# RWKV head pairs: both heads' A products and the two low-rank products on 64 rows of the array each

## The chip, the cores and the metric

The kernel runs on one core of a Trainium2 chip. The time is device microseconds of one execution. Engines are named as the profile names them: PE is TensorE, PEld its weight loads, DVE VectorE, ACT ScalarE, POOL GpSimd, SP SyncE. PSUM is the memory that matmuls write; a bank holds 512 fp32 values on each of 128 partitions.

## What is computed

One inference step of one decoder layer for 512 prompt tokens and 64 sample tokens (8 sequences of 8). RWKV-7 time mixing with 8 heads of 64 and differential attention with 4 heads run as parallel branches on the same normalised input, are merged by gates, and an MLP follows. The change lies in the RWKV branch:

```python
r, k, v, wd, ad, gd = jnp.split(Pr, RWKV_SPLITS, axis=-1)
w = -jax.nn.softplus(-(lp['w0'] + jnp.tanh(wd) @ lp['w2'])) - 0.5
decay = jnp.exp(-jnp.exp(w))
a = jax.nn.sigmoid(lp['a0'] + ad @ lp['a2'])
kk = hs(k * lp['k_k']); kk = kk / norm(kk)
k = k * (1.0 + (a - 1.0) * lp['k_a'])
# one step of the scan, for every head:
sa = einsum('bhij,bhj->bhi', S, -kk_t)
S = S * w_t + sa * (kk_t * a_t) + v_t * k_t
y_t = einsum('bhij,bhj->bhi', S, r_t)
```

`wd` and `ad` have 64 columns each. `w2` and `a2` are the two low-rank weights.

## The kernel before

The 576 tokens are 9 chunks of 64: eight of the prompt, one of the samples. Heads go in pairs; `rwkv(hp)` (L742 on) is a generator that prepares one head pair, `hp` 0 to 3, in stages. A tile has 128 partitions: 64 of the even head (`par` 0) and 64 of the odd head (`par` 1). `chain(pr)` (L987) then carries the state of two head pairs through the nine chunks (`pch`, `pY`). Below that run the dense products of the layer, the so-called fills: `ps_z`, `ps_g` and the like, products of 128x128 weights with 288 tokens. `fill` and `take` hand a given number of them to the PE between the steps of `rwkv`; the rest of the order comes from the scheduler that builds the program, which places each instruction by priority and by when it takes its inputs to be ready. Every engine then runs its instructions strictly in that order.

The steps that the texts name, in the order of one head pair:

- `pn`, `nr`, `nb` (L755 to L763): norms of `kk`. POOL raises `nr` to a power and copies it out to `nb`, which `pk` (L790) needs.
- `pw`, `pa` (L767 to L773): the low-rank products, in two halves of 288 tokens. `wl` holds w2 in rows 0 to 63 and zeros below; `al` holds zeros in rows 0 to 63 and a2 below. Both multiply the whole tile `Pt[12]`, which holds tanh(wd) above and ad below. ACT evacuates them into `u` and `aa`.
- DVE and ACT scans and products up to `rkp`, which `pbn` (L807) needs, and to `KB` and `ST` (L811 to L821). `KB` holds both heads, on their own partitions. `ST[par]` holds one head on its own 64 partitions; POOL sets the other 64 to zero (L818), so that a product over all 128 partitions sums that head alone.
- `pA` (L825 to L836): for each head nine products of `KB` with `ST[par]`, in groups of 4, 4 and 1 chunks, one bank for each group. DVE multiplies by masks: the head's own rows into `ABR`, the other rows into the zero half of `ST`.
- `pV` and `SVU`, `pK` and `KBt` (L843 to L855): transposes by PE, evacuated by ACT. POOL puts identity blocks and zeros into `SVU` and zeros into `TT` (L871, L872, L923, L924).
- `pI` (L861), then the inverse of a triangular block in 32x32 products (`pW`, `pZ`, L876 to L905), and `pF` (L937), which takes `vm`, made by POOL in three buffers.

PSUM: `bank` is a ring of three banks, `tbank` one, `cbank(0)` and `cbank(1)` one each (the chain's `pch` and `pY`), and two more belong to the fills.

Of the kernel before, what the change touches and what calls it, by code (L numbers as in the profile page):

```python
# [8 lines left out]
F32 = mybir.dt.float32  # L9
# [6 lines left out]
P = 128  # L16
# [25 lines left out]
def tile_hybrid_step(ctx, tc, xT, xsT, ktab, vtab, s0T, ptab, w_in, vecs, w2a2, g2, lamv,  # L42
                     w_bra, w_brb, w_out, w_up, w_down, cst, bias_p, bias_s,
                     yT, kTo, vTo, Sp, Ss, sh):
    nc = tc.nc
# [25 lines left out]
    def mm(out, lhsT, rhs, start=True, stop=True):  # L71
        ring["mm"] = PE.matmul(out=out, lhsT=lhsT, rhs=rhs, start=start, stop=stop)  # L72
        return ring["mm"]
# [27 lines left out]
    def bank(name):  # L101
        return psw.tile([P, 512], F32, tag="w", name=name)

    def tbank(name):
        return psc.tile([P, 512], F32, tag="t", name=name)
# [211 lines left out]
    ka2 = rc.tile([P, 8], F32, name="ka2")  # L317
    ts(ka2[:, 0:4], v(V_KA, 4), 0.5, MUL, 0.0, ADD, GE)
    ts(ka2[:, 4:8], v(V_KA, 4), -0.5, MUL, 1.0, ADD, GE)

    wl = rc.tile([P, 512], F32, name="wl")
    al = rc.tile([P, 512], F32, name="al")
    GE.memset(wl[64:128], 0.0)
    GE.memset(al[0:64], 0.0)
    wg = rc.tile([P, 512], F32, name="wg")
    reset = rc.tile([P, NT], F32, name="reset")
    GE.memset(reset, 1.0)
# [87 lines left out]
    with tc.issue_after(behind.ins):  # L415
        nc.sync.dma_start(out=pti, in_=ptab)
        nc.sync.dma_start(out=lv, in_=lamv)
        nc.sync.dma_start(out=bp, in_=bias_p)
        nc.sync.dma_start(out=bs, in_=bias_s)
        nc.sync.dma_start(out=wl[0:64], in_=w2a2[0:64])  # L420
        nc.sync.dma_start(out=al[64:128], in_=w2a2[64:128])
        nc.sync.dma_start(out=wg, in_=g2)

    def shifted(i):
# [317 lines left out]
    def rwkv(hp):  # L742
# [5 lines left out]
        def tmp(tag, bufs=1):  # L748
            return rt.tile([P, NT], F32, tag="T", name=f"{tag}_{hp}", bufs=6)
# [14 lines left out]
                       in_=nr.rearrange("p (a o) -> p a o", o=1).broadcast_to([P, 10, 64]))  # L764
        u = tmp("u")
        aa = tmp("aa")
        for t0, n in HALF:  # L767
            pw = bank(f"pw{hp}{t0}")
            mm(pw[:, :n], wl[:, hs], Pt[12][:, t0:t0 + n])
            act(u[:, t0:t0 + n], pw[:, :n], AF.Tanh, scale=0.5, bias=hw0[:, hp:hp + 1])  # L770
            pa = bank(f"pa{hp}{t0}")
            mm(pa[:, :n], al[:, hs], Pt[12][:, t0:t0 + n])
            act(aa[:, t0:t0 + n], pa[:, :n], AF.Tanh, scale=0.5, bias=hw0[:, 4 + hp:5 + hp])  # L773
        (fill if hp != 2 else take)(8)
        ts(u, u, 1.0, ADD)
# [38 lines left out]
        for par, rows in halves:  # L814
            stt(KB[rows, :, par], ch(aa)[rows], 0.5, ch(pinv)[rows], MUL, MUL)
            tt(KB[rows, :, 1 - par], ch(k2)[rows], ch(pinv)[rows], MUL)
            st = rb_.tile([P, NCH, 2, 64], F32, tag=f"ST{par}", name=f"ST{par}_{hp}")
            GE.memset(st[64 - 64 * par:128 - 64 * par], 0.0)  # L818
            stt(st[rows, :, 0], ch(kk)[rows], -1.0, ch(pm)[rows], MUL, MUL)
            tt(st[rows, :, 1], ch(r)[rows], ch(pe)[rows], MUL)  # L820
            ST.append(st)  # L821
# [1 line left out]


        ABR = rb_.tile([P, NCH, 2, 64], F32, tag="ABR", name=f"ABR{hp}")  # L825
        for par in range(2):
            rows = slice(64 * par, 64 * par + 64)
            oth = slice(64 - 64 * par, 128 - 64 * par)
            for c0, cn, mk in ((0, 4, C_M), (4, 4, C_M), (8, 1, C_MS)):
                pA = bank(f"pA{hp}{par}{c0}")  # L830
                for i in range(cn):
                    mm(pA[:, i * P:(i + 1) * P], KBc[c0 + i], ST[par][:, c0 + i])
                pAv = pA[:, :cn * P].rearrange("p (c w) -> p c w", c=cn)
                f2 = lambda a: a[:, c0:c0 + cn].rearrange("p c a t -> p c (a t)")
                tt(f2(ABR)[rows], pAv[rows], m3(c[rows, mk:mk + P], cn), MUL)
                tt(f2(ST[par])[oth], pAv[oth], m3(c[oth, mk:mk + P], cn), MUL)  # L836
# [647 lines left out]
```

## Time and profile before

| | |
|---|---|
| time, median of 3 | 1004.05 us (1003.92 to 1005.98) |
| profiled execution | 1006.88 us, of which its span 1005.1 us |
| mean granted TensorE clock | 0.993 |
| busy PE / PEld | 975.1 us (97%) / 919.4 us (91%) |
| busy DVE / ACT / POOL | 688.9 (69%) / 497.0 (49%) / 87.5 us (9%) |
| DMA | 105.75 MB, mean 105 GB/s |

The profile is that of one execution. Its page gives busy times, the chain that ended last and the costliest groups. Behind it stands the trace, which answers questions: what an engine did in a stretch (the timeline), who waited for whom (waits), and busy time, clock and DMA by stretch (windows). A timeline row gives start, duration of the merged group, engine, line, operation, out<-in, the tile of the PE array in rows*columns, and the shape. Each fp32 product of the RWKV steps is two records (passes) there, and their ends overlap, so the distance between starts, not the duration of one, is what a pass costs.

### The profile page before, as it was taken

What the parts mean: (1) busy time and instruction counts of PE and PEld (TensorE: products, weight loads), DVE (VectorE), ACT (ScalarE), POOL (GpSimd) and SP (SyncE); (2) the same over time, 40 slices, a digit from 0 to 9 for tenths busy, and PEclk for the clock granted to TensorE, in tenths of its full rate; (3) what the DMA queues carried; (4) which work ended last, traced back from release to release, by engine and by line L of the source; (5) the groups of instructions that cost most, each with busy time, mean ns of one, the idle gap of its engine ahead of it and who ended that gap; (6) DMA issues with size and microseconds to landing.
All of it is one profiled execution on the core that took longest, in us unless ns stands there. A gap on an engine that the chain in (4) does not pass through costs nothing.

```text
span 1005.1 us, 24415 instructions
## 1 busy us (share of the span) xinstructions
PE 975.1 (97%) x10012; PEld 919.4 (91%) x10012; DVE 688.9 (69%) x1459; ACT 497.0 (49%) x1094; POOL 87.5 (9%) x171
## 2 busy tenths in 40 slices
PE   9999999899999998999989999999999999999996
PEld 9999998898887887988779999999999999999996
DVE  6698566864946679444579898966666666666644
ACT  6576455354435355453334666644444444444732
POOL 2511001301010340000210000000000000000001
PEclk9999999999989999999999999999999999999999
DMA  7422673211111234323357642222222222221402
GB/s 266 136 70 83 205 223 114 61 64 45 43 59 45 69 106 152 104 81 113 103 182 225 206 140 86 83 95 85 88 92 85 85 84 85 84 87 41 135 3 95
DMA packets 50833, 105.75 MB, mean 105 GB/s; under 512 B 6066, under 2 KB 8114, under 8 KB 50594
## 3 DMA queue, kind: packets, MB, share of 16 engines
q1 hardware_dynamic: 47442, 96.95, 30.4%
q0 software_dynamic: 1648, 5.35, 1.5%
q8 instruction: 79, 1.29, 0.5%
q10 hardware_dynamic: 1632, 1.89, 0.5%
q14 instruction: 32, 0.26, 0.1%
HBM read 89.38 MB, written 14.78 MB: 104 GB/s over the span
## 4 chain that ended last, share of the span: by engine, by line
PE 83%; DVE 6%; ACT 4%; issue 3%; DMA 2%; POOL 1%; SPq 0%; DVEq 0%; ACTq 0%; POOLq 0%
PE ps_dn L72 20%; PE ps_g L72 8%; PE ps_z L72 8%; PE ua L1220 5%; PE ux L1220 5%; PE ps_wo L72 4%; PE ps_k L72 3%; PE uc L1220 3%; PE ub L1220 3%; PE ud L1220 2%; PE ps_bra L72 2%; PE ps_q L72 2%; PE pch L72 2%; PE ps_brb L72 2%; PE ps_v L72 2%
## 5 line engine op out<-in xcount | busy, mean ns | idle before, releaser
L72 PE MATMUL ps_dn<-q,hi_dn 128*128 128x288 f32 x768 | 154.7, 296 | 0.0
L72 PEld LDWEIGHTS ps_dn<-q,hi_dn 128*128 128x128 f32 x768 | 122.7, 188 | 1.4
L72 PE MATMUL ps_dn<-q,lo_dn 128*128 128x288 f32 x384 | 113.2, 295 | 0.0
L72 PE MATMUL ps_g<-xl,hi_g 128*128 128x288 f32 x256 | 79.7, 311 | 0.0
L72 PE MATMUL ps_g<-xh,hi_g 128*128 128x288 f32 x256 | 79.0, 309 | 0.0
L72 PE MATMUL ps_g<-xh,lo_g 128*128 128x288 f32 x256 | 79.0, 309 | 0.0
L72 PEld LDWEIGHTS ps_dn<-q,lo_dn 128*128 128x128 f32 x384 | 72.0, 188 | 0.0
L72 PE MATMUL ps_z<-xh,lo_z 128*128 128x288 f32 (+1 forms) x224 | 68.9, 308 | 0.0
L72 PE MATMUL ps_z<-xh,hi_z 128*128 128x288 f32 (+1 forms) x224 | 67.6, 302 | 0.0
L72 PE MATMUL ps_z<-xl,hi_z 128*128 128x288 f32 (+1 forms) x224 | 66.8, 298 | 0.0
L61 DVE TENSOR_TENSOR ya<-ya,ps_dn 128x288 f32<-128x288 f32 x96 | 43.2, 451 | 29.4 <-PE ps_dn L72 29.4
L58 ACT ACTIVATE hi_dn<-raw_dn 128x512 fp32r<-128x512 f32 x48 | 30.1, 628 | 57.0 <-PE ps_dn L72 57.0
L1220 PE MATMUL ua<-h_b,hi 128*128 128x288 f32 x256 | 53.2, 298 | 0.0
L1220 PE MATMUL ux<-h_t,hi 128*128 128x288 f32 x256 | 52.3, 296 | 0.0
L58 ACT ACTIVATE c<-c 128x288 f32<-128x288 f32 x112 | 48.4, 439 | 7.4 <-DVE c L61 5.8
L72 PEld LDWEIGHTS ps_g<-xh,hi_g 128*128 128x128 f32 x256 | 48.7, 190 | 3.1 <-issue 1.8
L72 PEld LDWEIGHTS ps_g<-xl,hi_g 128*128 128x128 f32 x256 | 48.6, 190 | 1.9
L72 PEld LDWEIGHTS ps_g<-xh,lo_g 128*128 128x128 f32 x256 | 48.6, 190 | 1.6 <-DVE lo_g L61 0.2
L58 ACT ACTIVATE hi<-a 128x1024 fp32r<-128x1024 f32 (+1 forms) x32 | 27.1, 846 | 42.0 <-PE ps_dn L72 34.2
L72 PE MATMUL ps_dn<-q,w 128*128 128x320 f32 (+1 forms) x336 | 46.3, 297 | 0.0
L61 DVE TENSOR_TENSOR lo<-s,hi 128x1024 fp32r<-128x1024 f32 x32 | 39.2, 1224 | 10.1 <-ACT hi L58 10.0
L72 PEld LDWEIGHTS ps_dn<-q,w 128*128 128x128 f32 x336 | 45.3, 190 | 0.1
(395 smaller groups left out, 2802.2 us busy)
## 6 DMA issues: line engine op xcount, KB each, us to landing
a<-in_w_up_dram SPq DMA_DIRECT2D x32, 512.0 KB, 3.4
raw_dn<-in_w_down_dram SPq DMA_DIRECT2D x64, 256.0 KB, 2.8
raw_g<-in_w_in_dram SPq DMA_DIRECT2D x32, 256.0 KB, 3.1
raw_z<-in_w_in_dram SPq DMA_DIRECT2D x28, 256.0 KB, 3.1
gt_d<-gg SPq DMA_DIRECT2D x16, 288.0 KB, 2.4
g<-gt_d SPq DMA_DIRECT2D x16, 288.0 KB, 3.6
kp<-in_ktab_dram SPq DMA_DIRECT2D x16, 256.0 KB, 4.5
vp<-in_vtab_dram SPq DMA_DIRECT2D x16, 256.0 KB, 3.8
```

What stands on the lines that cost most here:

```text
L58: ring["act"] = AE.activation(out=out, in_=in_, func=func, **kw)
L61: ins = (eng or VE).tensor_tensor(out=out, in0=a, in1=b, op=op)
L72: ring["mm"] = PE.matmul(out=out, lhsT=lhsT, rhs=rhs, start=start, stop=stop)
L1220: ring["mm"] = PE.matmul(out=ps[:, :288], lhsT=l[:, k], rhs=hb[blk][:, h, k], start=start and i == 0, stop=i == 11, skip_group_check=skip)
```

## The change

`wl` and `al` become one tile `wa`, loaded by one DMA, with no zeros. `pw` uses rows 0 to 63 of `wa` and `Pt[12]`, `pa` rows 64 to 127; the two are written in turn, `pa` to a bank of its own, and each is told to come after the product before it. For `pA` the loops change places: for each group of chunks, the products of both heads are written in turn, each on its own 64 rows of `KB` and `ST`, into two banks. The ring of three, `tbank` and both `cbank`s supply them. The zero memsets of `ST` go.

```diff
--- before.py
+++ after.py
@@ -317,11 +317,7 @@
     ka2 = rc.tile([P, 8], F32, name="ka2")
     ts(ka2[:, 0:4], v(V_KA, 4), 0.5, MUL, 0.0, ADD, GE)
     ts(ka2[:, 4:8], v(V_KA, 4), -0.5, MUL, 1.0, ADD, GE)
-
-    wl = rc.tile([P, 512], F32, name="wl")
-    al = rc.tile([P, 512], F32, name="al")
-    GE.memset(wl[64:128], 0.0)
-    GE.memset(al[0:64], 0.0)
+    wa = rc.tile([P, 512], F32, name="wa")
     wg = rc.tile([P, 512], F32, name="wg")
     reset = rc.tile([P, NT], F32, name="reset")
     GE.memset(reset, 1.0)
@@ -417,8 +413,7 @@
         nc.sync.dma_start(out=lv, in_=lamv)
         nc.sync.dma_start(out=bp, in_=bias_p)
         nc.sync.dma_start(out=bs, in_=bias_s)
-        nc.sync.dma_start(out=wl[0:64], in_=w2a2[0:64])
-        nc.sync.dma_start(out=al[64:128], in_=w2a2[64:128])
+        nc.sync.dma_start(out=wa, in_=w2a2)
         nc.sync.dma_start(out=wg, in_=g2)
 
     def shifted(i):
@@ -764,12 +759,15 @@
                        in_=nr.rearrange("p (a o) -> p a o", o=1).broadcast_to([P, 10, 64]))
         u = tmp("u")
         aa = tmp("aa")
+
         for t0, n in HALF:
             pw = bank(f"pw{hp}{t0}")
-            mm(pw[:, :n], wl[:, hs], Pt[12][:, t0:t0 + n])
+            nm = f"pa{hp}{t0}"
+            pa = bank(nm) if t0 == 0 else tbank(nm) if hp == 2 else cbank(1, nm)
+            for ps, rows in ((pw, slice(0, 64)), (pa, slice(64, 128))):
+                with tc.issue_after(ring["mm"].ins):
+                    mm(ps[:, :n], wa[rows, hs], Pt[12][rows, t0:t0 + n])
             act(u[:, t0:t0 + n], pw[:, :n], AF.Tanh, scale=0.5, bias=hw0[:, hp:hp + 1])
-            pa = bank(f"pa{hp}{t0}")
-            mm(pa[:, :n], al[:, hs], Pt[12][:, t0:t0 + n])
             act(aa[:, t0:t0 + n], pa[:, :n], AF.Tanh, scale=0.5, bias=hw0[:, 4 + hp:5 + hp])
         (fill if hp != 2 else take)(8)
         ts(u, u, 1.0, ADD)
@@ -815,7 +813,6 @@
             stt(KB[rows, :, par], ch(aa)[rows], 0.5, ch(pinv)[rows], MUL, MUL)
             tt(KB[rows, :, 1 - par], ch(k2)[rows], ch(pinv)[rows], MUL)
             st = rb_.tile([P, NCH, 2, 64], F32, tag=f"ST{par}", name=f"ST{par}_{hp}")
-            GE.memset(st[64 - 64 * par:128 - 64 * par], 0.0)
             stt(st[rows, :, 0], ch(kk)[rows], -1.0, ch(pm)[rows], MUL, MUL)
             tt(st[rows, :, 1], ch(r)[rows], ch(pe)[rows], MUL)
             ST.append(st)
@@ -823,14 +820,17 @@
 
 
         ABR = rb_.tile([P, NCH, 2, 64], F32, tag="ABR", name=f"ABR{hp}")
-        for par in range(2):
-            rows = slice(64 * par, 64 * par + 64)
-            oth = slice(64 - 64 * par, 128 - 64 * par)
-            for c0, cn, mk in ((0, 4, C_M), (4, 4, C_M), (8, 1, C_MS)):
-                pA = bank(f"pA{hp}{par}{c0}")
-                for i in range(cn):
-                    mm(pA[:, i * P:(i + 1) * P], KBc[c0 + i], ST[par][:, c0 + i])
-                pAv = pA[:, :cn * P].rearrange("p (c w) -> p c w", c=cn)
+
+        for c0, cn, mk in ((0, 4, C_M), (4, 4, C_M), (8, 1, C_MS)):
+            two = [cbank(par, f"pA{hp}{par}{c0}") if c0 == 4 else tbank(f"pA{hp}{par}{c0}")
+                   if c0 and par and hp < 3 else bank(f"pA{hp}{par}{c0}") for par in range(2)]
+            for i in range(cn):
+                for par, rows in halves:
+                    mm(two[par][:, i * P:(i + 1) * P], KB[rows, c0 + i].rearrange("p a t -> p (a t)"),
+                       ST[par][rows, c0 + i].rearrange("p a t -> p (a t)"))
+            for par, rows in halves:
+                oth = slice(64 - 64 * par, 128 - 64 * par)
+                pAv = two[par][:, :cn * P].rearrange("p (c w) -> p c w", c=cn)
                 f2 = lambda a: a[:, c0:c0 + cn].rearrange("p c a t -> p c (a t)")
                 tt(f2(ABR)[rows], pAv[rows], m3(c[rows, mk:mk + P], cn), MUL)
                 tt(f2(ST[par])[oth], pAv[oth], m3(c[oth, mk:mk + P], cn), MUL)
```

How the scheduler then orders the instructions is seen in the programs themselves. Numbers at the end of a name tell instances apart; `pA004` is head pair 0, head 0, chunks from 4 on; x4 are four products in a row.

On PE, head pair 0, at the A products, before:

```order
L72 MATMUL pA000_2825<-ST0_0_2814,KB0_2810 128x128 x4
L72 MATMUL pA004_2832<-ST0_0_2814,KB0_2810 128x128 x4
L72 MATMUL pA008_2839<-ST0_0_2814,KB0_2810 128x128
L72 MATMUL ps_z9_0_3032<-xh_103,lo_z9_1_3029 128x288
L72 MATMUL ps_z9_0_3032<-xh_103,hi_z9_1_3028 128x288
L72 MATMUL ps_z9_0_3032<-xl_104,hi_z9_1_3028 128x288
L72 MATMUL ps_z9_0_3032<-xh_103,lo_z9_1_3029 128x288
L72 MATMUL pA010_2843<-ST1_0_2820,KB0_2810 128x128 x4
L72 MATMUL ps_z9_0_3032<-xh_103,hi_z9_1_3028 128x288
L72 MATMUL ps_z9_0_3032<-xl_104,hi_z9_1_3028 128x288
L72 MATMUL ps_z9_0_3032<-xh_103,lo_z9_1_3029 128x288
L72 MATMUL pA014_2850<-ST1_0_2820,KB0_2810 128x128 x4
```

and after the change (`pA004` x4 stands alone, two `pbn` products and eight fills ahead of these rows):

```order
L72 MATMUL pA000_2819<-ST0_0_2810,KB0_2806 128x128 x4
L72 MATMUL ps_z5_1_2955<-xl_104,hi_z5_1_2950 128x296
L72 MATMUL ps_z5_1_2955<-xh_103,lo_z5_1_2951 128x296
L72 MATMUL ps_z9_0_3026<-xh_103,hi_z9_0_3018 128x288
L72 MATMUL ps_z9_0_3026<-xl_104,hi_z9_0_3018 128x288
L72 MATMUL ps_z9_0_3026<-xh_103,lo_z9_0_3019 128x288
L72 MATMUL ps_z9_0_3026<-xh_103,hi_z9_0_3018 128x288
L72 MATMUL ps_z9_0_3026<-xl_104,hi_z9_0_3018 128x288
L72 MATMUL pA010_2820<-ST1_0_2815,KB0_2806 128x128 x4
L72 MATMUL pA014_2834<-ST1_0_2815,KB0_2806 128x128 x4
L72 MATMUL pA008_2847<-ST0_0_2810,KB0_2806 128x128
L72 MATMUL pA018_2848<-ST1_0_2815,KB0_2806 128x128
```

The four-chunk groups of the two heads are not neighbours; only `pA008` and `pA018` are. In the other head pairs it is the same, with both four-chunk groups of one head in a row.

On PE, head pair 1, from the chain's first `pY` to the transposes `pK` and to `pI`, before:

```order
L72 MATMUL pY00_4570<-SVU0_2861,ST1_0_2820 64x64
L72 MATMUL pY00_4570<-SVU0_2861,ST0_1_3829 64x64
L72 MATMUL pY00_4570<-SVU0_2861,ST1_1_3835 64x64
L76 MATMUL pV1_448_3885<-cst_sb_75,P9_3086 128x128
L76 MATMUL pK10_3890<-cst_sb_75,KB1_3825 128x128 x4
L76 MATMUL pK14_3896<-cst_sb_75,KB1_3825 128x128 x4
L76 MATMUL pK18_3902<-cst_sb_75,KB1_3825 128x128
L72 MATMUL pI1_3915<-ST0_1_3829,s0_1_3905 64x16
```

and after the change, where thirteen fills stand between `pV1_448` and `pK10`, of which the last two are shown:

```order
L72 MATMUL ps_g8_0_4056<-xh_103,hi_g8_0_4048 128x288
L72 MATMUL ps_g8_0_4056<-xl_104,hi_g8_0_4048 128x288
L76 MATMUL pK10_3882<-cst_sb_75,KB1_3819 128x128 x4
L76 MATMUL pK14_3888<-cst_sb_75,KB1_3819 128x128 x4
L72 MATMUL ps_g8_0_4056<-xh_103,lo_g8_0_4049 128x288
L72 MATMUL ps_g8_0_4056<-xh_103,hi_g8_1_4052 128x288
L76 MATMUL pK18_3894<-cst_sb_75,KB1_3819 128x128
L72 MATMUL ps_g8_0_4056<-xl_104,hi_g8_1_4052 128x288
L72 MATMUL ps_g8_0_4056<-xh_103,lo_g8_1_4053 128x288
L72 MATMUL ps_g8_0_4056<-xh_103,hi_g8_1_4052 128x288
L72 MATMUL pI1_3907<-ST0_1_3823,s0_1_3897 64x16
```

The transposes and `pI` have moved away from the chain's `pch` and `pY` (which come twelve fills later) and stand among fills.

On POOL, head pair 0, around `nr` and `nb`, before:

```order
L818 MEMSET ST0_0_2814 64x1152
L818 MEMSET ST1_0_2820 64x1152
L760 TENSOR_TENSOR nr0_2749<-nr0_2749,mhalf_83 128x10
L871 COPY SVU0_2861<-cst_sb_75 64x64
L872 MEMSET SVU0_2861 64x64
L763 COPY nb0_2752<-nr0_2749 128x640
L871 COPY SVU0_2861<-cst_sb_75 64x64
L872 MEMSET SVU0_2861 64x64
L923 MEMSET TT0_3678 32x32
L924 MEMSET TT0_3678 32x9x32
L923 MEMSET TT0_3678 32x32
L924 MEMSET TT0_3678 32x9x32
```

and after the change (another `SVU` copy and memset stand right ahead of these rows):

```order
L871 COPY SVU0_2855<-cst_sb_75 64x64
L872 MEMSET SVU0_2855 64x64
L923 MEMSET TT0_3672 32x32
L924 MEMSET TT0_3672 32x9x32
L923 MEMSET TT0_3672 32x32
L924 MEMSET TT0_3672 32x9x32
L871 COPY SVU0_2855<-cst_sb_75 64x64
L872 MEMSET SVU0_2855 64x64
L871 COPY SVU0_2855<-cst_sb_75 64x64
L872 MEMSET SVU0_2855 64x64
L755 TENSOR_TENSOR nr0_2745<-nr0_2745,mhalf_83 128x10
L758 COPY nb0_2748<-nr0_2745 128x640
```

The memsets of `ST` are gone, and all the `SVU` and `TT` pieces now stand ahead of `nr` and `nb` instead of among and behind them.

## Rows read from the trace of the kernel before

**Rows 1.** The page: span, busy time by engine, the last chain by engine
```profile
span 1005.1 us, 24415 instructions
PE 975.1 (97%) x10012; PEld 919.4 (91%) x10012; DVE 688.9 (69%) x1459; ACT 497.0 (49%) x1094; POOL 87.5 (9%) x171
PE 83%; DVE 6%; ACT 4%; issue 3%; DMA 2%; POOL 1%; SPq 0%; DVEq 0%; ACTq 0%; POOLq 0%
```

**Rows 2.** Waits of PE, 170 to 490 us: total us, times, longest
```profile
PE pk L76 <- POOL nb L763: 2.7, 1, 2.7
PE pbn L72 <- DVE rkp L66: 2.6, 3, 1.8
...
PE pI L72 <- ACT KBt L58: 1.2, 2, 0.8
```

**Rows 3.** Four stretches: busy us (instructions) by engine, PEclk, DMA
```profile
core 0: us, PE busy (x) PEld busy (x) DVE busy (x) ACT busy (x) POOL busy (x), PEclk, DMA share, GB/s
177.00:184.00 7.00, 4.34 (x28) 3.78 (x27) 3.49 (x7) 3.21 (x6) 6.64 (x13) 1.00 0.08 20
270.00:277.00 7.00, 5.76 (x76) 4.85 (x74) 5.91 (x15) 5.48 (x15) 0.00 (x0) 0.98 0.01 2
277.00:284.00 7.00, 7.00 (x163) 5.90 (x162) 2.79 (x7) 1.91 (x6) 2.67 (x2) 0.53 0.01 2
```

**Rows 4.** Timeline of PE, head pair 0: A products and the next fills
```profile
195.93 2.22 PE L72 MATMUL pA<-ST,KB 128*128 128x128 f32 x18
197.90 0.38 PE L72 MATMUL ps_z<-xh,lo_z 128*128 128x288 f32 x1
```

**Rows 5.** Timeline of PE, head pair 0: low-rank products
```profile
176.49 0.65 PE L72 MATMUL pw<-P,wl 128*128 128x288 f32 x2
176.98 0.65 PE L72 MATMUL pa<-P,al 128*128 128x288 f32 x2
```

**Rows 6.** Timeline of PE: into a block of 32x32 tiles, out of 64x64 tiles
```profile
223.42 0.29 PE L72 MATMUL ps_z<-xl,hi_z 128*128 128x288 f32 x1
223.65 0.82 PE L72 MATMUL pW<-X,DM 32*32 32x32 f32 x72
...
304.80 0.45 PE L72 MATMUL pY<-SVU,ABR 64*64 64x64 f32 x8
305.17 0.41 PE L72 MATMUL ps_g<-xh,hi_g 128*128 128x288 f32 x1
305.42 0.29 PE L72 MATMUL ps_g<-xl,hi_g 128*128 128x288 f32 x1
305.55 0.30 PE L72 MATMUL ps_g<-xh,lo_g 128*128 128x288 f32 x1
```

**Rows 7.** Timeline of POOL, head pair 0
```profile
177.01 2.16 POOL L818 MEMSET ST<- 64x1152 f32 x2
179.14 2.18 POOL L760 TENSOR_TENSOR nr<-nr,mhalf 128x10 f32<-128x10 f32 x1
...
182.33 0.24 POOL L871 COPY SVU<-cst_sb 64x64 f32<-64x64 f32 x1
...
182.71 0.11 POOL L923 MEMSET TT<- 32x32 f32 x1
...
183.79 2.16 POOL L818 MEMSET ST<- 64x1152 f32 x2
```

**Rows 8.** Timeline of PE, end of head pair 1; in brackets idle before, and its releaser
```profile
273.40 1.20 PE L76 MATMUL pK<-cst_sb,KB 128*128 128x128 f32 x9 [0.43 <-ACT SVU L58]
275.41 1.11 PE L72 MATMUL pI<-ST,s 64*64 64x16 f32 x32 [0.81 <-ACT KBt L58]
276.45 2.05 PE L72 MATMUL pn<-cst_sb,sq 128*128 128x2 f32 x10
```

**Rows 9.** Timeline of PE, head pair 2: the first pF product pair and the second
```profile
351.38 1.08 PE L72 MATMUL pF<-vm,KBt 128*64 128x512 f32 x4
...
353.39 1.07 PE L72 MATMUL pF<-vm,KBt 128*64 128x512 f32 x3
```

**Rows 10.** Timeline of POOL in the same place: the fourth vm
```profile
352.60 1.05 POOL L61 TENSOR_TENSOR vm<-SVU,cst_sb 128x512 f32<-128x512 f32 x1 [1.70 <-PE pF L72]
```

**Rows 11.** Timeline of PE, norm products of head pair 3
```profile
365.47 1.28 PE L72 MATMUL pn<-cst_sb,sq 128*128 128x2 f32 x10
```

## The prediction

> **What bounds the kernel now.** I read the page first: TensorE (PE) is busy 97% of the span and holds 83% of the chain that ended last [rows 1]. So the time is the PE's instruction stream, and an edit counts only by the PE time or PE idling that it adds or removes. What can idle the PE lies in the RWKV part, so next come the waits of PE between 170 and 490 us [rows 2]: 2.7 us for POOL's `nb`, 2.6 us for VectorE's (DVE) `rkp` in three places, 1.2 us for ScalarE's (ACT) `KBt` before `pI`. Third, the stretches [rows 3]: from 277 to 284 us the granted clock averages 0.53, that is, TensorE runs mostly at 1.2 instead of 2.4 GHz. The stretch ahead of it, 270 to 277, has PE busy 5.76 of 7 us with small products; 177 to 184 is emptier (4.34 of 7) and keeps its full clock, so busy time alone does not decide. The sum is made against the profiled execution, 1006.88 us (span 1005.1 and 1.8 around it); the median, 1004.05, is 2.8 lower, and I subtract the same difference from both.
>
> **1. Halves at the same time: -4.3 us of PE work.** Every fp32 product is two passes. Nine chunks of `pA` for one half are 18 passes and take 1.97 us to the next fill [rows 4]: 0.11 us a pass, 0.22 a product, 72 products in all. If every product ran beside its other half, 36 x 0.22 = 7.9 us would go. The order printed above says otherwise. The scheduler has put all four-chunk groups of one half together and those of the other after them, with fills between; only the last chunks (`pA008` and `pA018`) stand next to each other. So for `pA` four pairs remain, 4 x 0.22 = 0.9 us. The low-rank products take 0.485 us each [rows 5]; they are adjacent in pairs for head pairs 0, 1 and 3 (two pairs each) and once for 2: 7 x 0.485 = 3.4 us. Bounds: 0 if 64-row products of 128 columns do not overlap, which no row of before shows, and -4.3. I take -4.3, by the nearest row: eight passes of 64x64 `pY` products, 64 columns each, are through in 0.37 us, tile change included [rows 6]; one after another, at half of the 0.11 that 128 columns take, they would need 0.44 without it.
> The Trainium skill ("TensorE: Matmul & The Clock Gate", Part 3, Measured speedup vs the span model) gives 3.07 times for four row tiles, less than the full four. By that share (an estimate: 0.77 of 4.3) the sum would be 1.0 us higher; the `pY` row shows no such loss.
>
> **2. Changes of tile size: +4.1 us.** Consecutive full-array products need none; before, `pA` and the low-rank products are full-array and go in and out without a seam (the fill after 18 passes starts at 197.90, on the pitch) [rows 4]. A 32x32 block starts 0.23 us after the fill ahead of it where fills follow each other by 0.13: +0.09 [rows 6]. Behind `pY` the next fill comes 0.37 us after the block's start, of which four pairs of passes are 0.22, so +0.15, and the fill behind that after 0.25 instead of 0.13: +0.12 [rows 6]. In and out cost 0.36 us; with 128 columns of weights in place of 64 I take 0.39, or 0.195 a change. Counted down the whole order, neighbours of unequal tile size are 21 more than before (three blocks of low-rank products, the separate `pA` groups of head pairs 0 to 3, less where they adjoin tiles anyhow): 21 x 0.195 = 4.1. Bounds: 2.0 (only the 0.09 each) and 5.9 (0.28 each, with a weight load in the open both ways).
> The Trainium skill has a rule that speaks against this change ("TensorEngine Tiling (Array Packing)", Key Properties): a change of tiling mode, not just of tile, drains TensorE. The rows agree in kind and give the size. If that drain were hidden behind queued work, this term would be zero and the sum 4.1 lower before cover.
>
> **3. What of both is covered.** The low-rank products stand ahead of a wait that another engine ends: `nb` for head pair 0 (2.66 us idle), `rkp` for 1 and 3 (2.6 us in three places) [rows 2]. PE arriving earlier there waits longer. So of -3.4 only head pair 2's -0.5 counts, and the +1.2 of the three blocks' six changes is hidden as well. Left: -0.9 - 0.5 = **-1.4**, and 4.1 - 1.2 = **+2.9**. Were the cover gone, -2.9 + 1.2 = -1.7 more.
>
> **4. POOL's zero halves: 0.** Eight memsets of 1.08 us go. For `nb` of head pair 0, two of them (2.16 us from 177.01) stood ahead of `nr` [rows 7]. In the new order the four `SVU` pairs (0.38 each, from 182.33 to 182.71) and the `TT` memsets (1.08, from 182.71 to 183.79) stand there: 2.6 us. `nb` comes at the same time within 0.5 us, hence no gain. Bounds -2.2 (they would be ready behind `nr` again) and +0.5. The single load in place of two runs long before its use: 0.
>
> **5. Head pair 1: waits -1.2.** The order printed above moves `pK` and `pI` away from the chain's first `pch`/`pY` and puts thirteen fills ahead of `pK` and three ahead of `pI`. So ACT has some 1.7 us (13 x 0.13) for the `SVU` copies that `pK` waited 0.43 for, and time for `KBt`, which `pI` waited 0.81 for [rows 8]. I take both as gone; bounds 0 and -1.2.
>
> **6. Head pairs 2 and 3: +1.0.** `pF0` and `pF1` had six fills between them; now all four products stand together. POOL's fourth `vm` needs a buffer that `pF0` frees, and took 1.05 us from 352.60, 0.14 after `pF0` [rows 9, 10]; the six fills (0.8 us) covered most of that. Now PE waits some 0.5 us. In head pair 3 the first `pA` group is reached 1.6 us earlier in the stream (seven fills, 0.9 us, and 32 of 36 `pW21` products, of which 36 take 0.8 [rows 6], fewer ahead of it), while DVE's order ahead of it is little changed; small waits, +0.5. Bounds -0.5 and +2.5 together.
>
> **7. The clock: -3.4.** The slow stretch of 6.8 us does work that takes half as long at full clock: ten `pn` products take 2.05 us there [rows 8] and 1.28 elsewhere [rows 11]; 7 us at 0.53 hold 3.3 us of loss [rows 3]. It began in the thin run `pY`, `pK`, `pI`, `pn`, with waits and hardly a fill. With sixteen fills moved into that run it should not begin. This is the least certain term: 0 if it stays, -3.4 if it goes.
>
> **Sum:** -1.4 + 2.9 + 0 - 1.2 + 1.0 - 3.4 = -2.1 us: 1004.8 for a profiled execution, **1002.0** for the median. Later stages are PE-bound and move along unchanged.
>
> **Rivals.**
> *The slow stretch stays.* For it: 64-row products put less on the array than the zero-padded ones did, and `pn` and the 32x32 blocks still follow. Against it: the fills. Term 7 is then 0 and the sum +1.3: 1005.3.
> *Slower: TensorE falls to 1.2 GHz in head pair 3 too.* There the new order has 3 `pW21`, `pA300`, `pA304`, 25 `pW21`, the second half's `pA` and 8 `pW21` in a row, where nine fills stood among them before. All of it is small tiles, behind a wait for `rkp`, as ahead of 277 us. It costs another 3.4 us if it lasts as long; the first stretch kept its length for the same cause. Sum -2.1 + 3.4 + 3.4 = +4.7: 1008.7. It decides from 4.1 us of loss over the forecast on; a second stretch alone, with the first one gone, ends at 1005.4.
> *All halves side by side.* If PE did overlap what the order keeps apart: -7.9 in place of -0.9 for `pA`, some six changes fewer (-1.2): 993.8. The order is fixed at build time and speaks against it.
> *Pairs do not overlap at all.* The -1.4 of step 3 is gone: 1003.4; little is lost, since cover hides the rest.
>
> **How the numbers follow.** Forecast 0.50; slow stretch stays 0.25; slower by a second stretch 0.15; no overlap 0.07; all side by side 0.03. A measurement of this kernel can tell about 0.2% (2.0 us) from no change. The forecast stands just past that edge: its own range, from the bounds of steps 2, 4 and 6, is 999 to 1004.5, and of its 0.50 I put 0.32 on faster and 0.18 on the same. With the others (0.05 of the second, 0.03 of the last faster; 0.16 and 0.04 the same): faster 0.40, same 0.38, slower 0.22. The range takes in the slow stretch staying and part of the slower rival: 998 to 1007.5.
>
> **What would show it.** Step 1: `pw` and `pa` start some ns apart, `pA` halves in separate runs. Step 2: seams of 0.1 to 0.2 us around every `pA` group. Step 3: PE's wait for `nb` grows to about 3 us, for `rkp` to over 3 in sum. Step 5: no waits of `pK` and `pI` in head pair 1. Step 6: `pF1` waits for POOL. Step 7: the granted clock between 270 and 285 us is 1.00. It is wrong if the clock falls anywhere new, or if `nb` moves.

## The result: slower by 0.4%, not faster by 0.2%

The changed kernel took 1010.08 us in the median (6 runs, 1007.68 to 1011.51) beside 1004.73 of the kernel before (6 runs): ratio 1.0045, 95% interval 1.0031 to 1.0059. Run again beside the kernel before it came to 1.0034 (1.0022 to 1.0046). Forecast were 1002.0 us and a range of 998 to 1007.5; the sign was wrong and the time lies outside.

The page of the changed kernel: span and busy time by engine.

```profile
span 1005.8 us, 24388 instructions
...
PE 973.5 (97%) x10012; PEld 915.8 (91%) x10012; DVE 688.8 (68%) x1459; ACT 496.3 (49%) x1094; POOL 80.2 (8%) x161
```

Against [rows 1] PE is busy 1.6 us less, POOL 7.3 less, and yet the span is 0.7 longer. This execution is the shortest of the six, and that of the kernel before (1006.88) is longer than any of the six timed beside it: two single profiles hide most of the difference. So the averages of all runs, further down, carry the account, and the profiles show only where things happen.

Waits of PE in the changed kernel, 170 to 490 us, which answer [rows 2]:

```profile
PE pk L76 <- POOL nb L758: 4.5, 1, 4.5
PE pZ L72 <- issue: 2.8, 4, 0.8
PE pbn L72 <- DVE rkp L66: 2.6, 2, 1.4
PE pK L76 <- ACT SVU L58: 1.0, 3, 0.4
PE pW L72 <- DVE X L884: 0.8, 1, 0.8
PE pZ L72 <- ACT W L58: 0.7, 2, 0.6
PE pW L72 <- issue: 0.5, 1, 0.5
...
PE pF L72 <- POOL vm L61: 0.3, 1, 0.3
...
PE pA L72 <- DVE ST L61: 0.2, 1, 0.2
```

The wait for `nb` has grown from 2.7 to 4.5 us. `rkp` costs the same 2.6. `pI`'s wait for `KBt` is gone. The waits around the inverse, of `pZ` and `pW`, sum to 4.8 us; in the kernel before they sum to 2.0:

```profile
PE pZ L72 <- issue: 1.5, 4, 0.9
...
PE pW L72 <- issue: 0.5, 1, 0.5
```

All waits of PE that the profile lists in this stretch sum to 14.2 us, beside 11.6 before.

The stretches of [rows 3] in the changed kernel, columns as there:

```profile
177.00:184.00 7.00, 2.52 (x18) 1.85 (x15) 2.17 (x3) 2.93 (x6) 6.04 (x15) 0.80 0.08 20
184.00:191.00 7.00, 7.00 (x41) 7.00 (x40) 4.81 (x11) 3.50 (x5) 0.00 (x0) 0.71 0.13 37
270.00:277.00 7.00, 6.73 (x73) 5.88 (x72) 6.05 (x13) 5.41 (x17) 0.00 (x0) 1.00 0.14 40
277.00:284.00 7.00, 6.15 (x190) 5.59 (x189) 4.99 (x15) 2.82 (x6) 2.78 (x2) 1.00 0.01 2
```

The stretch behind head pair 1 has its full clock, as forecast; a slow stretch now lies in and behind the wait for `nb`, where the kernel before had 1.00.

The low-rank products in the timeline of PE (start, duration, line, operation, tile, shape):

```profile
176.41 0.30 PE L72 MATMUL ps_z<-xh,hi_z 128*128 128x288 f32 x1
176.64 0.51 PE L72 MATMUL pw<-P,wa 64*128 64x288 f32 x1
176.65 0.51 PE L72 MATMUL pa<-P,wa 64*128 64x288 f32 x1
176.99 0.40 PE L72 MATMUL pw<-P,wa 64*128 64x288 f32 x1
...
177.47 0.40 PE L72 MATMUL pw<-P,wa 64*128 64x288 f32 x1
...
177.81 0.40 PE L72 MATMUL ps_z<-xl,hi_z 128*128 128x288 f32 x1
178.04 0.30 PE L72 MATMUL ps_z<-xh,lo_z 128*128 128x288 f32 x1
```

`pw` and `pa` start 0.01 us apart: they do run side by side. Around them lie the seams: 0.23 from the last fill instead of 0.13, 0.34 from the last pair to the next fill instead of 0.24, 0.23 to the one behind: +0.30, and another 0.1 behind the first pair.

### The profile page after: what moved, and what is told of

It is laid out like the page before. It is cut to its first block, busy times and chain, and to the rows that moved or that the text cites. A ratio compares the mean times of both kernels' runs of the same rounds, so it can differ in the third digit from the quotient of the medians.

```text
span 1005.8 us, 24388 instructions
## 1 busy us (share of the span) xinstructions
PE 973.5 (97%) x10012; PEld 915.8 (91%) x10012; DVE 688.8 (68%) x1459; ACT 496.3 (49%) x1094; POOL 80.2 (8%) x161
## 4 chain that ended last, share of the span: by engine, by line
PE 52%; ACT 2%; DVE 2%; issue 2%; POOL 1%; DMA 1%; DVEq 0%; SPq 0%; ACTq 0%; POOLq 0%
PE ps_dn L72 20%; PE ua L1220 5%; PE ux L1220 5%; PE ps_g L72 4%; PE ps_wo L72 4%; PE uc L1220 3%; PE ub L1220 3%; PE ud L1220 2%; PE ps_bra L72 2%; PE ps_brb L72 1%; PE pch L72 1%; PE pZ L72 1%; PE pY L72 1%; ACT oa L58 0%; PE pW L72 0%
```

## The experiments

The table puts all timed runs together. The kernel before has 106 runs beside the experiments: mean 1003.84 us, mean granted clock 0.9919 (the six beside the first series of the changed kernel, mean 1004.92, have no clock on record and are not among them). "At full clock" is the time times the mean granted clock, a bound on what a run would take had TensorE never been slowed. All differences are of means against the 106, with two standard errors; ratios are those of the comparison beside the kernel before. The two series of the changed kernel differ by 2.4 ± 1.6 us from each other, so a difference between series that did not run side by side is less sure than its interval says.

| kernel | runs | ratio, 95% interval | time, us | clock | at full clock, us |
|---|---|---|---|---|---|
| changed (twice) | 13 | 1.0045 (1.0031 to 1.0059), 1.0034 (1.0022 to 1.0046) | +4.8 ± 1.1 | 0.9910 | +3.8 ± 0.9 |
| e13, whole order, full rows | 9 | 1.0026 (1.0016 to 1.0036) | +2.4 ± 0.4 | 0.9937 | +4.1 ± 0.9 |
| e2 and e15, low-rank alone | 24 | 1.0025 (1.0014 to 1.0035), 1.0026 (1.0013 to 1.0038) | +2.7 ± 0.8 | 0.9890 | -0.2 ± 0.8 |
| e7 and e16, its order, full rows | 24 | 1.0014 (1.0002 to 1.0025), 1.0021 (1.0011 to 1.0031) | +1.6 ± 0.5 | 0.9910 | +0.7 ± 0.6 |
| e3, A products alone | 11 | 1.0009 (0.9997 to 1.0020) | +1.0 ± 1.0 | 0.9944 | +3.5 ± 1.2 |
| e6, its order, full rows | 12 | 0.9997 (0.9986 to 1.0009) | -0.3 ± 0.6 | 0.9939 | +1.8 ± 1.1 |
| e4, nb first | 9 | 1.0031 (1.0018 to 1.0043) | +3.5 ± 1.1 | 0.9921 | +3.7 ± 1.1 |
| e5, A side by side | 6 | 1.0051 (1.0031 to 1.0070) | +5.1 ± 1.5 | 0.9877 | +0.8 ± 0.9 |
| e8, A alone, side by side, nb first | 12 | 1.0020 (1.0006 to 1.0033) | +2.1 ± 1.1 | 0.9901 | +0.3 ± 1.0 |
| e9, before, nb first | 12 | 1.0013 (1.0001 to 1.0025) | +1.3 ± 0.9 | 0.9923 | +1.7 ± 1.0 |
| e10, as e8, other banks | 12 | 1.0022 (1.0011 to 1.0033) | +2.1 ± 0.7 | 0.9915 | +1.7 ± 1.1 |
| e11, low-rank queued pw, pw, pa, pa | 7 | 1.0052 (1.0033 to 1.0070) | +5.2 ± 1.6 | 0.9851 | -1.7 ± 1.7 |
| e12, all side by side, other banks | 6 | 1.0055 (1.0037 to 1.0072) | +6.2 ± 1.1 | 0.9833 | -2.5 ± 0.8 |
| e14, low-rank pairs twice | 6 | 1.0076 (1.0059 to 1.0093) | +7.0 ± 2.0 | 0.9897 | +4.7 ± 1.8 |

The column "at full clock" overcorrects, perhaps by half. Between runs of one and the same kernel (all 269 together) 0.001 less mean clock went with 0.44 ± 0.06 us more time, where the column takes 1.0. The profiles show two reasons. Each of the twenty ends in a slow stretch, 4.7 to 8.1 us of the span, in which PE has at most 0.8 us of work left. It lowers the mean clock, now more and now less, and costs next to nothing. In the kernel before it is this one:

```profile
1000.40:1005.10 4.70, 0.00 (x0) 0.00 (x0) 0.91 (x3) 0.00 (x0) 0.29 (x1) 0.50 0.67 223
```

And the waits that follow can hide a slow stretch. A second profile of the kernel before (e17, below) is slow for 3.4 us from 384.6 on, where the first is not:

```profile
384.00:388.00 4.00, 3.63 (x87) 3.21 (x88) 3.96 (x8) 1.76 (x3) 0.00 (x0) 1.00 0.91 275
```

```profile
384.00:388.00 4.00, 4.00 (x84) 3.61 (x82) 3.74 (x7) 1.78 (x3) 0.00 (x0) 0.58 0.76 262
```

Yet from `pV` of head pair 2 to `pV` of head pair 3 it takes 37.18 us, the first 37.03. In another place, from `pn` to `pC` at the end of head pair 1, a slow stretch of the same length made 23.51 us (e18) out of 21.96 (e1). So below, what goes by clock stands between 0.44 us for each 0.001 ("the lower price") and the column's 1.0.

**Is it the wait for nb?** The first theory was that POOL's later `nb` costs the time. e1 is the changed kernel again, e4 queues the `SVU` and `TT` pieces behind `nb` on POOL and leaves PE's order as it is, row for row.

```diff
+            with tc.issue_after(own["nb"].ins):
+                GE.tensor_copy(out=SVU[rows, 8, par], in_=...)
+                GE.memset(SVU[rows, 0, par], 0.0)
```

> The changed kernel once more, to see whether its times and its slow stretches repeat. POOL theory (the nb of head pair 0 comes 1.3 us later because POOL now does all SVU and TT pieces first, PE waits 4.5 us there, and TensorE falls to 1.2 GHz inside that wait): median 1008 to 1011 us, a wait of pk for nb of 4 to 5 us and a granted clock under 0.9 between 177 and 191 us again. Rival (changes of tile size and 64-row products cost it): the same median, and the slow stretch, if any, in another place.

> The changed kernel with one thing more: on POOL, the SVU and TT pieces of a head pair are queued behind that head pair's nb. PE's order is the same, instruction for instruction. POOL theory: nb is there at about 180 us instead of 183.6, PE's wait for it falls from 4.5 to at most 1.5 us, no fall of the clock in head pair 0, and 4 to 7 us go against the changed kernel: 0.996 to 1.000 of the kernel before. Rival (the cost lies in PE's own stream): within 2 us of the changed kernel, 1.003 or more.

e1 repeated the loss. In e4 the first effect came as expected, in PE's timeline:

```profile
181.19 0.66 PE L76 MATMUL pk<-cst_sb,nb 128*128 128x128 f32 x4 [2.01 <-POOL nb L758]
```

against, in the changed kernel,

```profile
183.62 0.69 PE L76 MATMUL pk<-cst_sb,nb 128*128 128x128 f32 x2 [4.48 <-POOL nb L758]
```

and its profile has no slow stretch there. But the time is that of e1 within the scatter (-0.1 ± 1.5 us): my theory fell. In this profile part of the gain is given back in head pair 2 (64.0 us from `pC` to `pV`, 61.8 in the changed kernel): PE waits 0.79 us for DVE, where the changed kernel waits 0.21 (idle in brackets), and a slow stretch from 348.1 to 351.5 us lengthens the rows. The wait for POOL's `vm`, 0.31, is that of the changed kernel.

```profile
346.75 2.99 PE L72 MATMUL pA<-ST,KB 64*128 64x128 f32 x20 [0.79 <-DVE ST L61]
```

e9 made the same edit, with the memsets of `ST` also behind `nb`, in the kernel before. There too an earlier `nb` won nothing (1.0013).

> The kernel before with nb of each head pair ahead of the ST, SVU and TT pieces on POOL; all products on full rows as before. If the wait for nb (2.7 us in the profile of the kernel before) is PE time that stays won, 0.996 to 0.999 of the kernel before; if it is given back further on, as it was with the changed kernel, 0.999 to 1.001.

**Which part of the change?** e2 has the low-rank products alone, e3 the A products alone.

> The kernel before with the low-rank products alone on 64 rows (one weight tile wa, pw and pa side by side, no zero halves of wl and al); A products and the zero memsets of ST as before. POOL theory: POOL's order around nb is as before, so no fall of the clock in head pair 0; seven pairs at the same time save at most 3.4 us of which waits swallow most: 0.997 to 1.001 of the kernel before. Rival: tile changes cost: 1.001 to 1.003.

> The kernel before with the A products alone on 64 rows each (two banks a group, zero memsets of ST gone); low-rank products as before, full array with zero halves. POOL theory: POOL's order around nb of head pair 0 is that of the changed kernel, so the wait for nb is 4 us or more, TensorE falls to 1.2 GHz behind it, and the time is 1.003 to 1.006 of the kernel before, as with the whole change. Rival: tile changes around the A products alone, some 12 of them: 1.001 to 1.003 and no fall of the clock there.

What the POOL theory said was wrong for both, the other way round: the low-rank products alone lose 2.7 us, the A products 1.0, which their interval does not tell from nothing. e3 speaks against the theory most plainly: its PE waits 3.9 us for `nb` and the clock falls behind it (0.88 from 177 to 191 us), and yet the time is not clear of the kernel before. e2 lies in its rival's range, but the table gives another reason than tile changes. The mean clock of the low-rank change is 0.0028 lower, which is 1.2 us of its loss at least, and all of it by the column (-0.2). The A products cost 3.5 at full clock, or 2.1 by the lower price, and their clock is 0.0025 higher, which returns part of it.

**Rows or order?** Each part moves instructions and also halves the rows. e6 and e7 take the loops, banks and queueing of one part but leave zero halves and full rows; e13 does so for both. e15 and e16 repeat e2 and e7 side by side.

```diff
-                    mm(two[par][:, i * P:(i + 1) * P], KB[rows, c0 + i]..., ST[par][rows, c0 + i]...)
+                    mm(two[par][:, i * P:(i + 1) * P], KBc[c0 + i], ST[par][:, c0 + i])
```

```diff
-            for ps, rows in ((pw, slice(0, 64)), (pa, slice(64, 128))):
-                    mm(ps[:, :n], wa[rows, hs], Pt[12][rows, t0:t0 + n])
+            for ps, wt in ((pw, wl), (pa, al)):
+                    mm(ps[:, :n], wt[:, hs], Pt[12][:, t0:t0 + n])
```

> The kernel before with the loops and banks of the changed A products, but full rows: ST keeps its zero half and every product uses all 128 rows. Nearly the order of the run with the A products alone, without its tile changes. Seam theory: time at full clock (time times mean granted clock) within 1.5 us of the kernel before, where the A products alone on 64 rows were 3.7 above it. Rival (order and banks, waits): 3 us or more above it as there.

> The kernel with the low-rank change alone, in the same order of PE and the same banks, but full rows with the zero halves kept: pw and pa one after the other. Theory (the clock falls behind the pairs of 64-row products): mean granted clock as in the kernel before, 0.991 to 0.993, against 0.989 with 64 rows; time 0.999 to 1.002 of the kernel before. Rival (the new order thins PE's work out, rows do not matter): mean clock 0.989 again and 1.002 or more.

> The low-rank change alone once more, beside the next run, to narrow the difference. If 64 rows lower the clock: mean clock 0.989, 1.002 to 1.003 of the kernel before.

> The same order of PE with full rows once more. If 64 rows lower the clock: mean clock 0.991, about 1 us faster than the run beside it. Rival (both are the same, the first difference was scatter): the same clock within 0.001 and the same time within 0.5 us.

> Loops, banks and queueing of the whole change, but every product on full rows with the zero halves kept. If the rows cost (tile changes, and the clock behind 64-row products): within 2 us of the kernel before, 0.999 to 1.002, mean clock 0.991 or more. If order and banks cost: 1.003 or more, as the change.

e7, e15 and e16 came out as the theory in their texts said. e6 (+1.8 at full clock) and e13 (1.0026) lie between the theory and the rival.

For the low-rank part the order of PE is the same in both kernels, but that with 64 rows the passes of `pw` and `pa` alternate. Together (24 runs each) 64 rows take 1.06 ± 0.88 us longer than full rows, at a clock lower by 0.0019 ± 0.0015, although each product pair needs about half the PE time. The profiles differ in two stretches, 241 to 252 and 364 to 376, around the low-rank products of head pairs 1 and 3 (columns as above). e2 and e15, 64 rows:

```profile
241.00:252.00 11.00, 11.00 (x125) 9.46 (x123) 5.96 (x13) 7.33 (x17) 4.05 (x6) 0.84 0.18 51
...
364.00:376.00 12.00, 12.00 (x103) 10.57 (x102) 6.80 (x14) 6.52 (x18) 7.10 (x8) 0.86 0.18 65
```

```profile
241.00:252.00 11.00, 11.00 (x113) 9.36 (x113) 5.40 (x11) 7.55 (x16) 3.51 (x6) 0.69 0.15 49
...
364.00:376.00 12.00, 10.84 (x94) 9.01 (x93) 5.68 (x14) 7.58 (x20) 5.24 (x4) 0.86 0.23 77
```

e7 and e16, full rows:

```profile
241.00:252.00 11.00, 11.00 (x132) 10.19 (x131) 5.87 (x12) 7.56 (x17) 4.05 (x6) 1.00 0.15 51
...
364.00:376.00 12.00, 12.00 (x111) 11.39 (x110) 6.80 (x14) 6.30 (x18) 7.11 (x8) 1.00 0.19 66
```

```profile
241.00:252.00 11.00, 11.00 (x123) 10.33 (x117) 5.97 (x13) 7.35 (x16) 4.05 (x6) 1.00 0.15 51
...
364.00:376.00 12.00, 12.00 (x99) 11.02 (x98) 6.80 (x13) 7.02 (x17) 7.10 (x8) 0.86 0.17 56
```

With 64 rows the clock fell in both places both times; with full rows in one of four. But it had fallen before the low-rank products of these head pairs began. In e15 the clock is down from 244.3 us on, and `pw` starts at 245.25:

```profile
244.30:245.20 0.90, 0.90 (x14) 0.60 (x8) 0.09 (x1) 0.86 (x3) 0.88 (x1) 0.50 0.00 0
```

```profile
245.25 0.85 PE L72 MATMUL pw<-P,wa 64*128 64x288 f32 x1
```

In the other three cases it fell 0.3, 0.7 and 1.4 us ahead of them. So these products did not set off the slow stretches that the windows show. Nor do the places belong to 64 rows: of all twenty profiles four fell between 241 and 252 us, one of them with full-row low-rank products (e9), and nine between 363 and 380, three of them with full rows (e6, e8, e16). In the three profiles of the changed kernel the first place never fell and the second once (0.86). That the mean clock is lower with 64 rows is what the series show; how it comes about they don't.

Against e13 the changed kernel is 2.4 ± 1.1 us slower, its clock 0.0027 ± 0.0016 lower. They did not run side by side: each against the kernel before beside it, 1.5 ± 1.1 us are left. Nor do they differ in rows alone, since e13 keeps the memsets of `ST` on POOL, and its PE waits 2.7 us for `nb`, not 4.5. And e13 itself, with full rows, is 2.4 us above the kernel before (2.7 ± 0.5 above the runs beside it), and 3.2 to 4.1 with its higher clock taken out: order and banks alone cost that, more than half of the loss. Its order is near that of the changed kernel, not equal to it.

**Where is the PE time of the order?** Once more a profile each of the kernel before (e17) and of the changed one (e18):

> The kernel before, profiled a second time. If its slow stretch behind head pair 1 belongs to the program: a granted clock under 0.8 between 276 and 285 us again. If it comes and goes: elsewhere or not at all.

> The changed kernel, profiled a third time. If the slow stretch in the wait for nb belongs to the program: a granted clock under 0.95 between 177 and 191 us for the third time, and none between 270 and 285.

Both were as expected for a stretch that belongs to the program, save that e18 has a short slow stretch behind head pair 1 too (second row of it). 177 to 191 and 270 to 285 us, e17, then e18:

```profile
177.00:191.00 14.00, 11.34 (x82) 10.89 (x82) 11.00 (x19) 6.77 (x12) 8.54 (x18) 1.00 0.14 45
270.00:285.00 15.00, 13.77 (x255) 11.78 (x258) 9.11 (x22) 7.51 (x20) 2.67 (x2) 0.77 0.01 3
```

```profile
177.00:191.00 14.00, 9.53 (x60) 9.21 (x59) 8.16 (x15) 6.02 (x11) 5.37 (x11) 0.88 0.09 26
270.00:285.00 15.00, 13.88 (x325) 12.32 (x323) 9.84 (x26) 7.09 (x20) 2.68 (x2) 0.89 0.11 36
```

The steady difference lies between `pC` of head pair 1 and `pV` of head pair 2, that is, the chain of the first two head pairs and the A products and `pF` of head pair 2. The clock was full there in all five profiles of the two kernels. First e17, then e18:

```profile
300.65 0.69 PE L72 MATMUL pC<-Y,Wc 32*32 32x32 f32 x32
...
359.08 0.71 PE L76 MATMUL pV<-cst_sb,P 128*128 128x128 f32 x5
```

```profile
299.93 0.69 PE L72 MATMUL pC<-Y,Wc 32*32 32x32 f32 x32
...
361.76 0.71 PE L76 MATMUL pV<-cst_sb,P 128*128 128x128 f32 x5
```

58.43 us against 61.83, with the same 199 fills in both; the other profiles give 58.43 and, twice, 61.84. Summed by the distance from each product's start to the next, the 3.4 us are: `pF` 2.33 to 3.25, `pA` 3.96 to 4.56, fills (the seams that they stand behind) 32.0 to 33.0, `pY` and `pch` 15.8 to 16.6, and low-rank products that came over from head pair 1, with `pk` and `pbn`, some 0.1. e13, with full rows, loses in the same place: 65.33 us, of which a slow stretch of 3.4 us explains 1.7 at most. Outside it, the waits of `pZ` and `pW` have grown in all three profiles of the changed kernel (4.8, 4.7 and 4.1 us between 170 and 490 us, against 2.0 and 1.2 before).

**Would the intended order have paid?** e5 queues the A products strictly in turn, so that all 36 pairs are neighbours.

```diff
-                for par, rows in halves:
-                    mm(two[par][:, i * P:(i + 1) * P], ...)
+                for par, rows in halves[::-1]:
+                    with tc.issue_after(ring["pA"] if c0 + i or not par else ring["mm"].ins):
+                        ring["pA"] = mm(two[par][:, i * P:(i + 1) * P], ...).ins
```

> The changed kernel with the A products of both halves queued strictly in turn (half 1, half 0, half 1, ...), so that all 36 pairs are neighbours in PE's order, 18 products of a head pair in one block. Seam theory (the changed kernel loses PE time because its four-chunk groups stand alone, each with a change of tile size on both sides and nothing beside it): 32 more pairs at the same time and fewer seams give back 7 to 9 us of PE time against the changed kernel, 0.995 to 0.999 of the kernel before. Rival (64-row products of 128 columns in two banks do not overlap, or the time goes into waits for DVE's masks): 1.002 or more.

```profile
199.21 2.28 PE L72 MATMUL pA<-ST,KB 64*128 64x128 f32 x36
203.21 0.63 PE L76 MATMUL pV<-cst_sb,P 128*128 128x128 f32 x4 [1.72 <-DVE ST L61]
```

36 passes are through in 2.28 us, where 18 took 2.22 before [rows 4]: the halves overlap wholly. With the lower clock taken out that is 1 to 3 us better than the changed kernel. But the pairs are done long before DVE's masks, and `pV`, next in the order, takes a bank that DVE still has to empty: 1.72 us back at once, 1.39 at `pF` in head pair 2. And the clock is lower again (0.9877); the time is no better. e8 is the same with full-row low-rank products and `nb` first; e10 gives the chain's banks to the first group, so that `pV` need not wait for it; e12 is e10 with the low-rank pairs.

> The A products alone on 64 rows, strictly in turn as in the side-by-side run, with nb ahead of the SVU and TT pieces on POOL, and low-rank products as before the change. Seam theory: the gain of the side-by-side run without the low-rank pairs' loss of clock: 0.993 to 0.998 of the kernel before, mean clock 0.993 or more. Rival: 1.000 or more.

> The run with the A products strictly in turn and nb first, low-rank products as before, with one change: the first group of A products goes to the chain's two banks instead of the second group, so that the banks that pV and pF take next are not those that DVE empties, and the order puts 17 to 28 fills between the A block and pV. Theory (the pairs' gain of some 8 us of PE time is real and went into waits of pV and pF for DVE's masks): those waits are gone, time at full clock 3 to 6 us below the side-by-side run with nb first, 0.993 to 0.998 of the kernel before. Rival (the gain is lost elsewhere, in seams or in the clock): 1.000 or more.

> The whole change with the A products strictly in turn, the first group in the chain's banks, and nb first. If the low-rank pairs lower the clock as they did alone: mean clock 0.002 to 0.003 below the same kernel with full-row low-rank products, and 1 to 3 us more time than it. Rival (low-rank pairs are harmless once PE's stream is dense): the same time within 1 us.

None is faster than the kernel before. e10 only moved the waits (3.1 us of `pA`, 2.4 of `pV` and 1.7 of `pF` on DVE's `ST`). e12 has the lowest mean clock of all (0.9833): by the column it lies 2.5 us below the kernel before and pays over 8 us in clock, by the lower price 2.4 above and pays 3.8. The low-rank change, rows and order together, puts it 4.1 ± 1.2 us above e10, at a clock lower by 0.0082, more of both than was expected. The stretch 290 to 460 us of e10, then of e12 (the profiled runs have mean clocks of 0.995 and 0.980, further apart than the kernels in the mean):

```profile
290.00:460.00 170.00, 158.38 (x2761) 135.21 (x2760) 102.90 (x232) 75.14 (x188) 17.74 (x30) 1.00 0.28 93
```

```profile
290.00:460.00 170.00, 160.39 (x2833) 137.77 (x2834) 106.54 (x234) 78.52 (x191) 17.52 (x30) 0.96 0.27 89
```

**Why is the clock lower with 64 rows?** Two kernels tried to tell the rows from PE's coming sooner to its waits.

> The low-rank change alone, but in the order pw, pw, pa, pa, so that only one of two pairs lies side by side and the block of 64-row products is longer. If 64-row products as such lower the granted clock: mean clock 0.989 or lower, as with the pairs; if it is the short block that brings PE sooner into its wait: 0.990 to 0.991, between the pairs and full rows.

> The low-rank change alone, with each pair of products issued twice into the same banks, so that PE is as long at work there as with full rows. If the clock falls because PE comes to its wait sooner: mean clock back at 0.991. If it falls because of 64-row products: 0.989 or lower, and 1.002 of the kernel before or more.

Neither decides. e11 was meant to have a longer block of 64-row products, but in head pairs 0 and 1 its halves run side by side all the same, and the block is as long as in e2 (1.18 us to the next fill, 1.17 there):

```profile
176.29 0.51 PE L72 MATMUL pw<-P,wa 64*128 64x288 f32 x1
176.30 0.51 PE L72 MATMUL pa<-P,wa 64*128 64x288 f32 x1
```

So its lower clock (0.9851) is not that of a longer block; `pbn` also stands 24 fills earlier in head pair 0. e14, with as much PE time as full rows, has 0.9897, but six runs leave ± 0.0036, which tells it neither from full rows (0.9910) nor from 64 (0.9890). It differs from e2 in more than the low-rank products from head pair 1 on, and its loss is mostly not clock. That question stays open; that the kernels with the low-rank pairs have the lower mean clock is what e2, e15, e7 and e16 show.

## Why the prediction was wrong, step by step

Without the clock the forecast was +1.3 us, with it -2.1. Measured are +4.8 ± 1.1: +0.4 to +0.9 by clock, the other 3.8 to 4.4 without it. Two steps failed by about as much as each other: step 7, which counted on a gain by clock that did not come, and steps 4 to 6, which took the new order to cost nothing. Both signs that the prediction named for being wrong are there: the clock falls in a new place, and `nb` moves.

- **Step 1** was right in its mechanism: pairs start 0.01 us apart, and those of `pA` overlap wholly (e5). It was right that the order keeps `pA` apart.
- **Step 2** was right in kind: seams of 0.1 us at each end and behind each end, 0.4 in and out of a low-rank block, where 0.39 was taken. `pA`, measured as the distance from each product's start to the next, cost more with 64 rows (4.37, 4.18, 4.56 and 4.18 us by head pair, in the changed kernel) than with full ones (3.97, 3.72, 3.96, 4.09) in spite of its four pairs.
- **Steps 1 to 3 together** said +1.5. The changed kernel against e13 says -0.3 ± 1.2 at full clock and +1.2 by the lower price, with the differences beside rows that are named above: no sign of a large error here, but no measurement of these steps alone either.
- **Step 3**: the cover by `nb` was named rightly: PE came to it 0.5 us earlier and waited that much longer. The waits for `rkp`, which were to grow to over 3 us, stayed at 2.6.
- **Step 4** said no change for `nb`, 0.5 at most. POOL reaches `nr` 1.7 us later (179.14 [rows 7], 180.80 now); 1.1 of that is two small copies ahead of it, which took 0.40 and 1.20 us where [rows 7] has 0.24 for one. The longer wait is real, but e4 shows that the time does not hang on it.
- **Step 5** was right for `pI`, whose wait is gone; `pK` still waits, 1.0 us in three places.
- **Steps 4 to 6 together** said -0.2. e13, which has order and banks without the 64 rows, stands at +2.4 ± 0.4 us, and at +3.2 to +4.1 with its clock taken out. I had costed head pair 2's `pF` at 0.5, where it measured 0.9. I had not costed the waits of `pZ` and `pW` in head pairs 1 and 3 (+2.8 us in the first pair of profiles), nor that DVE and POOL in head pair 2 follow a PE that has fewer fills between its blocks: e13 idles 2.0 us before its second `pA` half there (the long row behind it runs partly at the lower clock).

```profile
346.93 4.10 PE L72 MATMUL pA<-ST,KB 128*128 128x128 f32 x20 [2.00 <-DVE ST L61]
```

- **Step 7** failed, and with it the sign. The slow stretch behind head pair 1 did go or shorten, in three of three profiles. But I took every other place to keep its clock, and one profile for the rule. A gain of 3.4 us by clock would be a mean clock 0.0034 higher; it is 0.0009 ± 0.0015 lower, +0.4 to +0.9 us in place of -3.4. In all three profiles a new slow stretch lies at the wait for `nb` (0.76, 0.88 and 0.88 from 177 to 191 us). e13, with full rows, has a mean clock 0.0018 ± 0.0008 above the kernel before, so its order is worth 0.8 to 1.8 us of clock, not 3.4. Why the changed kernel lacks even that is not shown: 64 rows and POOL's later `nb` both set it apart from e13.

The slower rival was right that TensorE would run at 1.2 GHz in a new place, and came nearest by its time, 1008.7 us; but it named the wrong place (the small tiles of head pair 3) and had a chance of 0.15. Its reason, that 64-row products put less on the array, is neither shown nor ruled out: a slow stretch at the wait for `nb` stands in the profiles of e6 and e7 too, which have full rows.

The rule that I had set beside step 2 (the Trainium skill, "TensorEngine Tiling (Array Packing)", Key Properties: a change of tiling mode drains TensorE) agrees with the seams of 0.1 us on either side of the low-rank pairs. The measured 3.07 times of four row tiles (the Trainium skill, "TensorE: Matmul & The Clock Gate", Part 3, Measured speedup vs the span model) was no limit here: two tiles of 64 rows gave the full two, 36 passes in the time of 18.

## What to carry to other kernels

A slow stretch of TensorE in one profile is not a stock of time that an edit can collect: compare mean clocks over many runs, ask where an edit may slow TensorE next, and price a slow stretch by what the next wait leaves of it (0.15 us of 3.4 in one place here, 1.55 in another). Before calling work the cause of a slow stretch, look whether it starts ahead of it. Side-by-side tiles pay only if the order brings them together, if the engine that empties their banks keeps up, and if what they save is not in front of a wait; here all three failed in turn. To price a reordering, run it once with the old arithmetic: e13, e6 and e7 told the cost of the order, which no single profile did; run it beside the kernel that it is compared with.

## What the hardware showed that was not expected

Two kernels with nearly the same order, PE just as busy in the stretch, had different clocks there: 0.84 and 0.69 with 64-row low-rank products, 1.00 twice with full rows (241 to 252 us), though the fall came before these products. A slow stretch of 3.4 us cost 1.55 us in one place and 0.15 in another. And POOL's copy of 64x64 values, 0.24 us in the kernel before [rows 7], took 1.20 us while DVE ran a scan, and ended with it. POOL, then DVE, in the changed kernel:

```profile
178.90 0.40 POOL L871 COPY SVU<-cst_sb 64x64 f32<-64x64 f32 x1
...
179.43 1.20 POOL L871 COPY SVU<-cst_sb 64x64 f32<-64x64 f32 x1
...
180.80 1.99 POOL L755 TENSOR_TENSOR nr<-nr,mhalf 128x10 f32<-128x10 f32 x1
```

```profile
178.74 0.46 DVE L69 TENSOR_SCALAR u<-u 128x576 f32<-128x576 f32 x1 [2.74 <-ACT u L58]
179.24 1.36 DVE L775 TENSOR_TENSOR_SCAN cum<-reset,u 128x576 f32<-128x576 f32 x1
```

The same two durations stand in the other two profiles of the changed kernel (0.39 and 1.20). The Trainium skill ("GPSIMD Engine Reference", 1. Specifications) says that GpSimd shares its SBUF interfaces with VectorE and contends with DVE instructions that have two SBUF inputs; the scan has two, and the rows agree, 1.20 us for 0.24. That the scan holds POOL up was not tried by itself.
